# Second token half of x loaded a second time, transposed, with its root spread by one product, in a hybrid decoder layer

## The chip, the cores and the metric

The kernel runs on one core of a Trainium2 chip. The core has a matrix engine (TensorE, "PE" in the profile, with its weight loads as "PEld"), three engines for elementwise work (VectorE "DVE", ScalarE "ACT", GpSimd "POOL"), and queues that start transfers between device memory and the on-chip memory (here mostly that of SyncE, "SP"). Matrix products are written to a small accumulator memory, PSUM, of eight banks of 128x512 f32; everything else lies in SBUF, a memory of 128 partitions. The metric is device time of one execution in microseconds; the median of three runs is 1091.97 us (1091.26 to 1092.28).

## The reference

One decoder layer on x of 1024 tokens and width 1024 in float32. Cut to what matters here:

```python
h = rmsnorm(x, pre_w_mix) * (1.0 + sc1) + sh1          # sh1, sc1: columns of silu(c) @ w_ada + b_ada
proj = h @ w_in                                         # attention q, k, v and four recurrent inputs
aq, ak, av, hq, hf, hi, hg = split(proj)
attn = rmsnorm(window_attention(rope(aq), rope(ak), av, sinks), attn_out_w)
rec  = rmsnorm(hgrn2(silu(hq), 1 - f, hi, log f), hg_norm_w) * silu(hg)
x = x + g1 * rmsnorm(concat(attn, rec) @ w_out, post_w_mix)
# then a second sub-layer: a dense MLP of width 4096 with squared ReLU, normalised and modulated alike
```

`rmsnorm` divides a token's row by the root of its mean square, and `sc1`, `sh1` are one number per column of the width, the same for all tokens.

## The kernel before

**Tiles.** Tokens are cut into eight blocks of 128 (`tb`), in two halves `th` of four blocks each. The width is cut into eight blocks of 128 (`kb`). A product over the width needs h with the width on the partitions, while x arrives with tokens on the partitions. So each half is first multiplied row by row with its root (`norm_scale`, L207, one instruction for a token block and a half of the width), then transposed by TensorE against the identity (`first_T`, L215: four 128x128 transposes into one PSUM bank for a `kb`), and then taken out of PSUM by `split_evac` (L223). The matrix products run in a format with a shortened mantissa, so every factor is split into a high part and a rest, and a product is three matmuls (high x high, high x rest, rest x high). `split_evac` makes this split in a chain of three engines: ScalarE writes `hhi = a*xT + s` (a and s are the modulation's columns), GpSimd forms `f = hhi - s`, and VectorE writes `hlo = a*xT - f`.

**Order.** All compute instructions go through the helper `Queue` (L28), whose issuing line is L39; so all rows of the profile bear L39. While an engine is pinned (`pin(True, ...)`, L358, until L697), each instruction is tied behind the one issued before it on that engine: the engine's queue has the order of the program text. Behind L697 the framework's scheduler orders freely, but nothing gets ahead of the last pinned instruction.

**First half.** The loop over `kb` from 1 to 7 (L464) does for each block of the width: `first_evac` of the first half; `first_wq`, `first_wql`, `first_kv`, which split the weights of q and of k, v; the products `first_mm(kb, tb, part)` for token blocks 0 to 3, part 0 with hhi and part 1 with hlo, into the banks pq0 to pq3 and two shared banks for k and v; and `first_T` of the next block. Between them come the columns of the modulation: `mod_sum` (L309) adds a weight tile times a number of c on VectorE (rows `macc`), `mod_turn` (L318) transposes the sum on TensorE (rows `pmt`, in the bank of `a_ps`), reduces it and writes the columns that the next blocks' `split_evac` read. At `kb == 3` SP's queue gets the loads of token blocks 4 to 7, two tiles for a block (a half of the width each): eight loads of 256 KB. Their squares (`norm_sq`, rows `jx`, ScalarE) follow at `kb` 5 and 6, the root (`norm_rstd`) at 6, the row scalings at 6 and 7, the first two transposed blocks of the second half at 7.

**PSUM.** `tp_ps` hands out five banks, `mm_ps` two and `a_ps` one. During the first half four of the five and both of `mm_ps` hold sums; one of the five is left for transposes, and `a_ps` serves the modulation.

**Second half.** A loop at L678 and L682 issues `first_evac(1, kb, first_T(1, kb))`, the copies of the finished q blocks (`qproj`) and of k, v (`kvproj`), and the products of token block 4's q (`pq4`), three steps behind the evacuations. Then come the rotations (`rope`) and, from L730, a list of sixteen pieces (`filler`): q and k, v of token blocks 4 to 7 and the values of the recurrent part, between which the attention steps of the token blocks are placed. Attention of block 0 begins before piece 4, that is behind the q and k, v products of blocks 4 and 5.

Of the kernel before, what the change touches and what calls it, by code (L numbers as in the profile page):

```python
# [47 lines left out]
def hybrid_layer(ctx: ExitStack, tc: tile.TileContext, I, out, dbg=None):  # L48
# [40 lines left out]
    def mm_ps(name):  # L89
        return pmm.tile([P, 512], F32, tag="mm", name=name)  # L90
# [124 lines left out]
    def first_T(th, kb, mk=tp_ps):  # L215
        pst = mk(f"xT{th}_{kb}")
        hf, col = kb // 4, (kb % 4) * P
        for j in range(4):
            PE.transpose(pst[:, j * P:(j + 1) * P], xh[th * 4 + j][hf][:, col:col + P], ident)
        return pst  # L220
# [147 lines left out]
    def idle(n):  # L368
        for _ in range(n):
            PE.matmul(spare_ps, lhsT=ones_r, rhs=spare, start=True, stop=True)  # L370
# [6 lines left out]
    def first_rows(*js):  # L377
        for j in js:
            PE.transpose(xT0[0][:, j * P:(j + 1) * P], xh[j][0][:, 0:P], ident)
# [31 lines left out]
    def first_wql(kb):  # L411
        hi, lo = wq[kb]
        DVE.tensor_tensor(lo, wqr[kb], hi.bitcast(F32), ALU.subtract)
# [26 lines left out]
    norm_scale(0, 0, ACT, (3,))  # L440
    idle(4)
    mod_mm((0, 1), range(2))
    first_rows(2)
    idle(1)
    first_rows(3)
    mod_mm((0, 1), range(2, 4))
    mod_copy((0, 1))
    first_part(1)
# [5 lines left out]
        first_mm(0, tb, 0, (0,))  # L454
    mod_fold((0, 1))
    first_wql(1)
    for tb in (2, 3):
        first_mm(0, tb, 0, (1,))
    xT0.append(first_T(0, 1))
    for tb in (2, 3):  # L460
        first_mm(0, tb, 1)

    nextq = {1: (1, 0)}
    for kb in range(1, KB):  # L464
        q = nextq.get(kb)
        first_evac(0, kb, xT0[kb])
        if kb + 1 < KB:
            first_wq(kb + 1)
        if kb == 3:
            norm_scale(0, 1, ACT)  # L470
            pin(True, SP)
            for hf in range(2):
                for tb in range(4, TB):
                    load_x(tb, (hf,))
            pin(False, SP)
        first_mm(kb, 0, 0)
        first_mm(kb, 1, 0)
        if q:
            mod_mm(q)
            mod_copy(q)  # L480
        first_mm(kb, 2, 0)
        if kb in (3, 5):
            mod_turn((kb // 2 + 1, 0))
        first_mm(kb, 3, 0)
        if kb + 1 < KB:
            first_wql(kb + 1)
        if q:
            mod_fold(q)
        if kb == 2:
            mod_sum((2, 0), (2, 6, 3, 7))  # L490
        if kb == 4:
            mod_sum((3, 0), (5, 2, 6, 3, 7))
        if kb in (1, 3, 5):
            first_kv((kb + 1) // 2, DVE)
        if kb == 1:
            mod_sum((2, 0), (0, 4, 1, 5))
        if kb == 3:
            mod_sum((3, 0), (0, 4, 1))
        if kb + 1 < KB:
            xT0.append(first_T(0, kb + 1))  # L500
        if kb in (5, 6):
            for tb in range(4, TB):
                norm_sq(tb, (kb - 5,))
        if kb == 6:
            norm_rstd(1, 0, 4)
            norm_scale(1, 0, DVE)
        if kb == 7:
            norm_scale(1, 1, DVE)
        if kb == KB - 1:
            xT1 = [first_T(1, 0), first_T(1, 1, a_ps)]  # L510
        for tb in range(4):
            first_mm(kb, tb, 1)

# [8 lines left out]
    def htok(tb):  # L522
        sl = slice(tb % 4 * P, tb % 4 * P + P)
        return [(hh[k][tb // 4][0][:, sl], hh[k][tb // 4][1][:, sl]) for k in range(KB) if hh[k][tb // 4]]
# [6 lines left out]
    sinT = cload("sinT", [P, TB, 16], pool=XA)  # L531

    def qproj(tb):
        if tb < 5:
            pq = pq0[tb]
        else:
            pq = mm_ps(f"pq{tb}")
            proj3(pq, htok(tb), wq)
        q = m_(f"q{tb}")
        if tb in (0, 1):  # L540
            DVE.tensor_scalar(q, pq, 0.125, None, ALU.mult)
        else:
            ACT.activation(q, pq, AF.Copy, scale=0.125)
        qn.append(q)

    def kvproj(tb):
        if tb < 4:
            pk = pk0[tb]
        else:
            pk = mm_ps(f"pk{tb}")  # L550
            proj3(pk[:, :256], htok(tb), wkv)
        kv = XA.tile([P, 256], F32, tag="kv", bufs=8, name=f"kv{tb}")
        if tb < 4:
            DVE.tensor_copy(kv, pk[:, :256])
        else:
            ACT.activation(kv, pk[:, :256], AF.Copy)
        kvn.append(kv)

    def rope(tb, nh, eng=POOL):
# [115 lines left out]
            next(att[tb])  # L675

    att = [attention(tb) for tb in range(TB)]
    for kb in range(2):  # L678
        qproj(kb)
        first_evac(1, kb, xT1[kb])  # L680
    pq0.append(mm_ps("pq4"))
    for kb in range(2, KB + 3):  # L682
        if kb < KB:
            first_evac(1, kb, first_T(1, kb, mm_ps if kb == 2 else tp_ps))
        if kb == 2:
            qproj(2)
            qproj(3)
        if kb == KB:
            for tb in range(4):
                kvproj(tb)  # L690
        if kb > 2:
            proj3(pq0[4], htok(4)[kb - 3:kb - 2], wq[kb - 3:kb - 2], kb == 3, kb == KB + 2)
    for tb in range(4):
        eng = DVE if tb < 2 else POOL
        rope(tb, 8, eng)
# [1046 lines left out]
def layout(x, c, w_ada, b_ada, pre_w_mix, w_in, attn_sinks, attn_out_w, lb_table,  # L1742
           hg_norm_w, w_out, post_w_mix, pre_w_mlp, w_up, w_down, post_w_mlp):
    A = {}
    f = lambda a: np.ascontiguousarray(a)
    cols = lambda v: f(np.asarray(v).reshape(-1, P).T)
    A["x"] = f(np.asarray(x)[0])
    t_cT = cols(np.asarray(c)[0])
    wa = np.asarray(w_ada)[0]
    w1 = wa[:, :2048]  # L1750
    A["wada1"] = f(w1.reshape(4, 2, P, 2, 4, 256).transpose(3, 4, 0, 2, 1, 5).reshape(2, 4, 4, P, 512))
    A["wada1"][:, 2:] = (w1.reshape(2, 4, P, 2, 4, 256)[:, :, :, :, 2:].transpose(0, 4, 1, 2, 3, 5)
                         .reshape(2, 2, 4, P, 512))
    A["wada1"][:, 0] = (w1.reshape(2, 2, 2, P, 2, 8, P)[:, :, :, :, :, :2].transpose(1, 5, 0, 3, 4, 2, 6)
                        .reshape(2, 4, P, 512))
    A["wada"] = f(wa.reshape(KB, P, 6, 2, 512).transpose(2, 3, 0, 1, 4))
    ba = np.asarray(b_ada)[0]
    t_bT = cols(ba)
    A["b_g1"] = f(ba[2048:3072])
    A["b_g2"] = f(ba[5120:6144])  # L1760
    t_prew1 = cols(np.asarray(pre_w_mix)[0])
    t_prew2 = cols(np.asarray(pre_w_mlp)[0])
    A["postw1"] = f(np.asarray(post_w_mix)[0])
    A["postw2"] = f(np.asarray(post_w_mlp)[0])
    wi = np.asarray(w_in)[0]
    perm = [0, 4, 1, 5, 2, 6, 3, 7]
    A["w_q"] = f(wi[:, :512].reshape(D, 8, 64)[:, perm].reshape(KB, P, 512))
    A["w_kv"] = f(wi[:, 512:768].reshape(4, 2, P, 256).transpose(0, 2, 1, 3).reshape(4, P, 512))
    A["w_hv"] = f(wi[:, 1792:2304].reshape(KB, P, 512))
    hd = np.stack([wi[:, 1280:1792], wi[:, 768:1280], wi[:, 2304:2816]])  # L1770
    A["w_hd"] = f(hd.reshape(3, KB, P, 4, P).transpose(3, 0, 2, 1, 4).reshape(4, 3, P, D))
    sk = np.asarray(attn_sinks)[0]
    order = [0, 1, 4, 5, 2, 3, 6, 7]
    A["sinks"] = f(np.broadcast_to(sk[order], (P, 8)))
    A["attw"] = f(np.asarray(attn_out_w)[0].reshape(8, 64)[perm].reshape(4, P).T)
    A["lbt"] = f(np.asarray(lb_table).reshape(2, 4, P).transpose(2, 0, 1))
    A["hgw"] = f(np.asarray(hg_norm_w)[0].reshape(P, 1))
    wo = np.asarray(w_out)[0]
    A["w_o"] = f(np.concatenate([wo[:512].reshape(8, 64, D)[perm].reshape(4, P, D), wo[512:].reshape(4, P, D)]))
    A["w_u"] = f(np.asarray(w_up)[0].reshape(KB, P, 32, P).transpose(2, 1, 0, 3).reshape(32, P, D))  # L1780
    A["w_dn"] = f(np.asarray(w_down)[0].reshape(32, P, D))
    A["tab"] = f(np.concatenate([np.eye(P, dtype=np.float32), t_cT, t_bT, t_prew1, t_prew2], 1))
    inv = (np.float64(500000.0) ** (-np.arange(0, 16, 2) / 16.0)).astype(np.float32)
    ang = (np.arange(1024, dtype=np.float32)[:, None] * inv[None, :]).astype(np.float64)
    co, si = np.cos(ang).astype(np.float32), np.sin(ang).astype(np.float32)
    A["cosT"] = f(np.concatenate([co, co], 1).reshape(TB, P, 16).transpose(1, 0, 2))
    A["sinT"] = f(np.concatenate([-si, si], 1).reshape(TB, P, 16).transpose(1, 0, 2))
    i = np.arange(P)
    A["mle"] = (i[None, :] <= i[:, None]).astype(np.int32)
    A["fle"] = (i[:, None] <= i[None, :]).astype(np.float32)  # L1790
    si_, ti = i[:, None], i[None, :]
    A["hmask"] = (si_ <= ti).astype(np.int32)
    A["rmask"] = f(np.broadcast_to((np.arange(512) % CH != 0).astype(np.float32), (P, 512)))
    return A
# [14 lines left out]
```

## Time and profile before

| | |
|---|---|
| runs | 1091.26, 1091.97, 1092.28 us (median 1091.97) |
| profiled execution, its own time | 1091.43 us |
| its span in the profile | 1089.5 us |
| granted TensorE clock | 0.998 |
| PE busy | 1072.7 us, 98% |
| DVE busy | 803.2 us, 74% |
| ACT busy | 586.2 us, 54% |
| POOL busy | 373.0 us, 34% |
| bytes moved | 203.63 MB in the span |

A row of the time-ordered view has the start in us, the duration, engine, line, operation, the tile written and the tiles read, the shape, the count; in brackets stands how long the engine was idle before and what ended that. A row of the chain of waits has start, duration, engine and tile. A row of the windows has for each engine the busy time in the window and the number of instructions (PE, PEld, DVE, ACT, POOL), then the granted clock, the DMA share and GB/s. Matmuls overlap their neighbours, so the time between starts says more than a matmul's own duration.

### The profile page before, as it was taken

Reading aid. Unit: us, or ns where it says so; the run is one execution under the profiler, and the core shown is the slowest. Engines: PE = TensorE matmul, PEld = TensorE weight load, DVE = VectorE, ACT = ScalarE, POOL = GpSimd, SP = SyncE. Lnnn points to the kernel's source line nnn. Section 1 sums busy time; section 2 is a strip of 40 time slices with the busy share of each in tenths; the row PEclk is TensorE's granted clock in tenths of the full one; section 3 lists DMA queues with packets and bytes.
Section 4 is the critical chain, followed back from the end, with each engine's and each line's share of the span. In section 5 each row is a group of like instructions: output and inputs, shape, how many; then the busy total and the mean of one; then the engine's idle time right before and its main releaser. Section 6 shows DMA issues by size and latency. Waiting matters only on the chain.

```text
span 1089.5 us, 16106 instructions
## 1 busy us (share of the span) xinstructions
PE 1072.7 (98%) x5480; PEld 875.2 (80%) x5480; DVE 803.2 (74%) x1336; ACT 586.2 (54%) x1207; POOL 373.0 (34%) x497
## 2 busy tenths in 40 slices
PE   8999999999999999999999999999999999999996
PEld 6888666788888888888888888888888888888885
DVE  4867768878865564559777767776777787899786
ACT  4535553454565754566655555556664544466435
POOL 1263211143234653432444434444333334300014
PEclk9999999999999999999999999999999999999999
DMA  9701201544310252324577776767999888998538
GB/s 359 264 20 65 92 1 59 167 130 124 115 59 30 88 196 85 135 87 137 194 248 244 234 258 213 264 232 248 315 377 300 274 287 276 321 303 272 172 95 140
DMA packets 101826, 203.63 MB, mean 187 GB/s; under 512 B 13040, under 2 KB 13808, under 8 KB 101744
## 3 DMA queue, kind: packets, MB, share of 16 engines
q1 hardware_dynamic: 86256, 155.04, 41.9%
q0 software_dynamic: 15200, 47.20, 14.4%
q8 instruction: 43, 0.70, 0.3%
q14 instruction: 39, 0.32, 0.1%
q10 hardware_dynamic: 288, 0.36, 0.1%
HBM read 147.51 MB, written 55.05 MB: 186 GB/s over the span
## 4 chain that ended last, share of the span: by engine, by line
PE 90%; DVE 4%; DMA 2%; ACT 1%; POOL 1%; issue 1%; DVEq 0%; SPq 0%; POOLq 0%; ACTq 0%
PE pda L39 16%; PE pua L39 14%; PE pdc L39 8%; PE po L39 8%; PE puc L39 7%; PE pu L39 4%; PE pdb L39 4%; PE phg L39 4%; PE phq L39 3%; PE pub L39 3%; PE phf L39 3%; PE pv L39 3%; PE pq L39 3%; PE pk L39 1%; PE o L39 1%; PE sc L39 1%
## 5 line engine op out<-in xcount | busy, mean ns | idle before, releaser
L39 POOL TENSOR_TENSOR b<-b,b 128x512 f32<-128x512 f32 x64 | 88.7, 1386 | 216.4 <-DMA b<-w_dn 216.0
L39 ACT ACTIVATE dw<-dwr 128x512 fp32r<-128x512 f32 x72 | 45.4, 631 | 53.2 <-DMA dwr<-td 30.1
L39 ACT ACTIVATE s<-s 128x512 f32<-128x512 f32 x84 | 53.0, 631 | 31.8 <-DVE s L39 30.5
L39 DVE TENSOR_TENSOR acc<-pda,acc 128x512 f32<-128x512 f32 x68 | 46.7, 686 | 19.6 <-PE pda L39 19.2
L39 DVE TENSOR_TENSOR dw<-dwr,dw 128x512 fp32r<-128x512 f32 x72 | 53.1, 737 | 5.8 <-ACT dw L39 5.7
L39 POOL TENSOR_TENSOR rrf<-ssf,mhalf 128x1 f32<-128x1 f32 x7 | 7.6, 1081 | 105.5 <-DVE ssf L39 105.5
L39 POOL DMA_DIRECT2D td<-b x64 | 36.4, 568 | 19.0 <-POOL b L39 19.0
L39 ACT ACTIVATE s<-pua 128x512 f32<-128x512 f32 x28 | 16.7, 597 | 40.2 <-PE pua L39 37.4
L39 ACT ACT_TABLE_LOAD x28 | 35.9, 1283 | 1.7 <-PEq L1802 1.2
L39 DVE TENSOR_TENSOR wt<-a,wt 128x512 fp32r<-128x512 f32 x42 | 35.3, 841 | 0.9 <-ACT wt L39 0.9
L39 DVE TENSOR_TENSOR wt<-s,wt 128x512 fp32r<-128x512 f32 x42 | 34.2, 814 | 2.3 <-ACT wt L39 2.2
L39 DVE SCALAR_TENSOR_TENSOR macc<-wada,cs,macc 128x512 f32<-128x512 f32 x42 | 33.6, 800 | 3.1 <-DMA wada<-wada 2.6
L39 POOL DMA_DIRECT2D b<-w_dn x64 | 34.5, 541 | 2.7 <-issue 2.7
L39 POOL TENSOR_TENSOR comb<-comb,rd 128x512 f32<-128x512 f32 x8 | 11.7, 1458 | 63.3 <-DVE rd L39 44.2
L39 PE MATMUL pua<-bt_0h,wt 128*128 128x512 f32 x84 | 32.7, 389 | 0.0
L39 PE MATMUL pua<-bt_1h,wt 128*128 128x512 f32 x84 | 32.7, 389 | 0.0
L39 PE MATMUL pua<-bt_2h,wt 128*128 128x512 f32 x84 | 32.7, 389 | 0.0
L39 PE MATMUL pua<-bt_3h,wt 128*128 128x512 f32 x84 | 32.7, 389 | 0.0
L39 ACT ACTIVATE wt<-s 128x512 fp32r<-128x512 f32 x42 | 26.3, 627 | 7.6 <-DVE s L39 7.4
L39 DVE TENSOR_TENSOR acc<-pdc,acc 128x512 f32<-128x512 f32 x36 | 24.6, 684 | 7.2 <-PE pdc L39 7.0
L39 PE MATMUL pda<-dw,du_6h 128*128 128x512 f32 x96 | 29.6, 389 | 0.0
L39 PE MATMUL pdc<-dw,du_3h 128*128 128x512 f32 x96 | 29.5, 389 | 0.0
(766 smaller groups left out, 3746.5 us busy)
## 6 DMA issues: line engine op xcount, KB each, us to landing
dur<-ud SPq DMA_DIRECT2D x112, 256.0 KB, 4.4
wada<-wada SPq DMA_DIRECT2D x64, 256.0 KB, 3.6
b<-w_dn POOLq DMA_DIRECT2D x64, 256.0 KB, 5.2
td<-b POOLq DMA_DIRECT2D x64, 256.0 KB, 3.4
dwr<-td SPq DMA_DIRECT2D x64, 256.0 KB, 4.4
a<-w_u SPq DMA_DIRECT2D x56, 256.0 KB, 4.5
dwr<-w_dn SPq DMA_DIRECT2D x48, 256.0 KB, 4.3
ud<-s SPq DMA_DIRECT2D x42, 256.0 KB, 3.4
```

What stands on the lines that cost most here:

```text
L39: ins = op(*args, **kw)
```

## The change

The input is laid out twice: besides `x`, device memory holds `xT1`, the second token half with the width on the rows, as eight tiles of 128x512. The kernel loads these eight tiles (256 KB each) on SP's queue at `kb` 5 and 6 and no longer transposes or scales the rows of token blocks 4 to 7. The untransposed tiles of these blocks are still loaded, since their squares give the root. The root, one number for a token, now has to be multiplied along the free dimension: VectorE writes `dgx`, the identity times the root, four 128x128 blocks; one product of a matrix of ones with it puts the root of each of the 512 tokens on every partition (`rbx`, in PSUM); and VectorE multiplies each `xT1[kb]` with it in place, just ahead of that block's `first_evac`.

With that come a new order in the first half: the transposes of block 1 stand one group of products earlier; blocks 3, 5 and 7 of the width are transposed into the bank of `a_ps`; the modulation's sums are dealt out otherwise over the blocks (the last of gate 2 at `kb == 3`); one warming product is left out; six of the eight squares stand at `kb` 5 and two at 6. In the second half the loop has one form for all eight blocks: product, evacuation, one copy of q or k, v (all on ScalarE now), and the three matmuls each of token blocks 4 and 5, where pq5 stood among the pieces behind.

```diff
@@ -440,9 +440,7 @@
-    first_rows(2)
-    idle(1)
-    first_rows(3)
+    first_rows(2, 3)
...
     first_wql(1)
+    xT0.append(first_T(0, 1))
     for tb in (2, 3):
         first_mm(0, tb, 0, (1,))
-    xT0.append(first_T(0, 1))
...
-        first_mm(kb, 0, 0)
-        first_mm(kb, 1, 0)
+        if kb == 3:
+            mod_sum((2, 0), (7,))
+        if kb in (3, 5):
+            first_wql(kb + 1)
+        for tb in range(3):
+            first_mm(kb, tb, 0)
+            if kb == 7 and tb == 1:
+                rbx = tp_ps("rbx")
+                PE.matmul(rbx, lhsT=ones, rhs=dgx.rearrange("p a t -> p (a t)"), start=True, stop=True)
         if q:
             mod_mm(q)
             mod_copy(q)
-        first_mm(kb, 2, 0)
         if kb in (3, 5):
             mod_turn((kb // 2 + 1, 0))
         first_mm(kb, 3, 0)
-        if kb + 1 < KB:
+        if kb not in (3, 5) and kb + 1 < KB:
             first_wql(kb + 1)
...
-        if kb == 2:
-            mod_sum((2, 0), (2, 6, 3, 7))
-        if kb == 4:
-            mod_sum((3, 0), (5, 2, 6, 3, 7))
...
-        if kb == 1:
-            mod_sum((2, 0), (0, 4, 1, 5))
-        if kb == 3:
-            mod_sum((3, 0), (0, 4, 1))
+        if kb < 5:
+            mod_sum(*{1: ((2, 0), (0, 4, 1)), 2: ((2, 0), (5, 2, 6, 3)),
+                      3: ((3, 0), (0, 4, 1)), 4: ((3, 0), (5, 2, 6, 3, 7))}[kb])
         if kb + 1 < KB:
-            xT0.append(first_T(0, kb + 1))
+            xT0.append(first_T(0, kb + 1, a_ps if kb in (2, 4, 6) else tp_ps))
+        for tb, hf in {5: ((4, 0), (5, 0), (6, 0), (7, 0), (4, 1), (5, 1)), 6: ((6, 1), (7, 1))}.get(kb, ()):
+            norm_sq(tb, (hf,))
         if kb in (5, 6):
-            for tb in range(4, TB):
-                norm_sq(tb, (kb - 5,))
+            for j in range(4 * kb - 20, 4 * kb - 16):
+                xT1.append(load_raw(hT_ if j < 6 else m_, f"xT1_{j}", I["xT1"][j]))
         if kb == 6:
             norm_rstd(1, 0, 4)
-            norm_scale(1, 0, DVE)
-        if kb == 7:
-            norm_scale(1, 1, DVE)
-        if kb == KB - 1:
-            xT1 = [first_T(1, 0), first_T(1, 1, a_ps)]
+            dgx = t_("dgx", (P, 4, P))
+            DVE.tensor_tensor(dgx, ident.unsqueeze(1).broadcast_to([P, 4, P]),
+                              rx[1].unsqueeze(2).broadcast_to([P, 4, P]), ALU.mult)
...
-    for kb in range(2):
-        qproj(kb)
+    pq0.append(a_ps("pq4"))
+    for kb in range(KB):
+        DVE.tensor_tensor(xT1[kb], xT1[kb], rbx, ALU.mult)
         first_evac(1, kb, xT1[kb])
-    pq0.append(mm_ps("pq4"))
-    for kb in range(2, KB + 3):
-        if kb < KB:
-            first_evac(1, kb, first_T(1, kb, mm_ps if kb == 2 else tp_ps))
-        if kb == 2:
-            qproj(2)
-            qproj(3)
-        if kb == KB:
-            for tb in range(4):
-                kvproj(tb)
-        if kb > 2:
-            proj3(pq0[4], htok(4)[kb - 3:kb - 2], wq[kb - 3:kb - 2], kb == 3, kb == KB + 2)
+        (qproj if kb < 4 else kvproj)(kb % 4)
+        if kb == 0:
+            pq0.append(mm_ps("pq5"))
+        for tb in (4, 5):
+            proj3(pq0[tb], htok(tb)[kb:kb + 1], wq[kb:kb + 1], kb == 0, kb == KB - 1)
...
+    A["xT1"] = f(np.asarray(x)[0, 512:].T.reshape(KB, P, 512))
```

More of the change, by code (lines that the diff above doesn't have):

```diff
@@ L463, in hybrid_layer @@
     nextq = {1: (1, 0)}
+    xT1 = []
     for kb in range(1, KB):
@@ L533, in qproj @@
     def qproj(tb):
-        if tb < 5:
+        if tb < 6:
             pq = pq0[tb]
@@ L539, in qproj @@
         q = m_(f"q{tb}")
[L540 to L543, printed above, removed]
+        ACT.activation(q, pq, AF.Copy, scale=0.125)
         qn.append(q)
@@ L552, in kvproj @@
         kv = XA.tile([P, 256], F32, tag="kv", bufs=8, name=f"kv{tb}")
[L553 to L556, printed above, removed]
+        ACT.activation(kv, pk[:, :256], AF.Copy)
         kvn.append(kv)
```

## The prediction, made before the result was known

> **What bounds the kernel now.** I read the page first (busy shares), then the stages by window, then the chain of waits between 53 and 81 us, and last the time-ordered rows of each engine in that stretch.
>
> ```profile
> span 1089.5 us, 16106 instructions
> PE 1072.7 (98%) x5480; PEld 875.2 (80%) x5480; DVE 803.2 (74%) x1336; ACT 586.2 (54%) x1207; POOL 373.0 (34%) x497
> ...
> 45.00:50.00 5.00, 4.42 (x28) 3.79 (x28) 4.24 (x11) 3.38 (x10) 0.83 (x1) 1.00 0.28 90
> 55.00:60.00 5.00, 4.66 (x34) 4.10 (x33) 4.09 (x8) 2.03 (x3) 1.37 (x2) 1.00 0.00 0
> ...
> 100.00:110.00 10.00, 9.64 (x79) 7.86 (x78) 9.25 (x20) 4.89 (x16) 3.83 (x7) 1.00 0.45 152
> 110.00:120.00 10.00, 8.80 (x67) 6.32 (x67) 7.58 (x18) 5.67 (x21) 3.43 (x7) 1.00 0.64 217
> 125.00:200.00 75.00, 73.50 (x432) 51.66 (x429) 58.47 (x121) 33.05 (x110) 13.07 (x18) 1.00 0.14 44
> ```
>
> TensorE is the bound: 16.8 us of idle in the whole span (1089.5 − 1072.7). A microsecond taken from it, or put into it as a wait, before 200 us moves the end by about that much, except for what the idle time of the attention stage gives back: 0.36 + 1.20 + 1.50 = 3.1 us in the last three rows. The changed stretch, in the chain of waits:
>
> ```profile
> 53.89 0.46 PE pq L39 x2
> ...
> 56.68 0.87 PE xT L39 x8
> ...
> 57.90 0.23 PE pq L39
> ...
> 66.58 0.76 DVE hlo L39
> 67.34 0.04 issue
> 67.39 1.20 PE pq L39 x4
> 68.58 2.88 PE pk L39 x24
> 71.46 5.46 PE pq L39 x24
> 76.92 2.87 PE pk L39 x24
> 79.80 0.44 PE pqT L39 x4
> ```
>
> At 53.89 block 7 of the first half begins; eight transposes for the second half follow at 56.68 (six more groups of four come up to 65). pq4 ends at 68.58, then kv4 (2.88), pq5 (5.46), kv5 (2.87), and attention starts at 79.80. Without kv4, "pq4 and pq5 are done" would stand at 76.92 − 2.88 = **74.04**; in the changed kernel kv4 comes after both, so this is the point to compare.
>
> **The change, part by part.** *Removed from TensorE:* 32 transposes. By the row of 56.68, eight take 0.87: 4 × 0.87 = 3.48 us. Also one warming product of 0.23 (the step from 16.45 to 16.68 in the chain):
>
> ```profile
> 16.45 0.23 PE spare L39
> 16.68 0.12 PE xT L39
> ...
> 1079.05 1.02 PE L39 MATMUL pdly<-x,c_tab 128*128 128x512 f32 x2
> ```
>
> *Added to TensorE:* the product that spreads the root, 128x512 with plain f32 operands; no row before has that form with `ones`, the last row is the same shape and type: 1.02 busy, of which I take 0.95 as its step. Bounds 0.47 (two passes at the 0.23 of an fp32r matmul) and 1.02. On work alone the change is worth 3.48 + 0.23 − 0.95 = 2.8 us. pq5 only moves.
>
> *The eight row scalings* leave VectorE, but eight products of the same size come in, `xT1[kb] * rbx`. What decides is where they stand. The loop issues, for each kb: the product (VectorE), hhi (ScalarE), f (GpSimd), hlo (VectorE). VectorE is pinned there, so the product of kb+1 sits in its queue behind hlo of kb, and hlo of kb waits for f, f for hhi, hhi for the product of kb. Nothing of kb+1 can begin before kb is through. Today VectorE has only hlo in this chain, and the transposes run ahead. These rows show that the queue does keep its order, and what each link takes:
>
> ```profile
> 57.82 0.69 DVE L39 TENSOR_SCALAR q<-pq 128x512 f32<-128x512 f32 x1 [0.59 <-PE pq L39]
> 58.83 0.75 DVE L39 SCALAR_TENSOR_TENSOR hlo<-xT,a,f 128x512 fp32r<-128x512 f32 x1 [0.32 <-POOL f L39]
> 59.50 0.68 DVE L39 TENSOR_SCALAR q<-pq 128x512 f32<-128x512 f32 x1
> ...
> 61.02 0.75 DVE L39 SCALAR_TENSOR_TENSOR hlo<-xT,a,f 128x512 fp32r<-128x512 f32 x1 [0.18 <-POOL f L39]
> ...
> 105.75 0.67 DVE L39 TENSOR_TENSOR q<-q,rb 128x512 f32<-128x512 f32 x1
> ...
> 59.42 0.78 ACT L39 ACTIVATE hhi<-xT,sh,a 128x512 fp32r<-128x512 f32 x1 [0.82 <-PE xT L39]
> ...
> 60.29 0.69 POOL L39 TENSOR_SCALAR f<-hhi,ns 128x512 f32<-128x512 f32 x1 [0.82 <-ACT hhi L39]
> ...
> 33.06 2.55 ACT L39 ACTIVATE x<-x,r_x 128x512 f32<-128x512 f32 x4
> ```
>
> VectorE stood 0.32 us before the hlo of 58.83 while the copy queued behind it, q1, had its sum finished already (last pq1 matmul, 57.90 + 0.23 = 58.13 in the chain): an in-order queue. The period of one kb: product 0.67 (the row of 105.75, same shape with one operand in PSUM) + 0.02 of handing over; hhi until f starts 60.29 − 59.42 = 0.87 from PSUM, and since xT1 now lies in SBUF, where four scalings took 2.55 (0.61 each, against a step of about 0.67), I take 0.80; f until hlo 61.02 − 60.29 = 0.73; hlo until the next VectorE instruction 59.50 − 58.83 = 0.67. Together **P = 2.89 us**, eight times: 7 × 2.89 + (0.69 + 0.80 + 0.73 + 0.76 + 0.04) = 20.23 + 3.02 = **23.25 us**. TensorE's work in it is 48 matmuls of 5.46 / 24 = 0.23, 1.4 us a kb: it stands idle half of each period, and being pinned too, with kv4 and kv5 behind the loop, has nothing to fill in.
>
> *Where the chain starts.* The product with `ones` stands in block 7 behind two token blocks (each two pq and two pk matmuls, 0.46 + 2 × 2.88 / 24 = 0.70), so, if block 7 begins as before at 53.89, the first VectorE product starts at 53.89 + 1.40 + 0.95 = **56.24**, hlo of block 7 being done by then. End of the chain 56.24 + 23.25 = 79.49; four matmuls remain after the last hlo, 1.20 by the row of 67.39: **80.69**. Against 74.04: **+6.65 us**.
>
> *That block 7 begins as before* is a term of its own. The reordering takes waits away from TensorE and brings two:
>
> ```profile
> 20.64 0.50 PE L39 MATMUL pq<-wq1h,hhi 128*128 128x512 f32 x1 [0.17 <-ACT hhi L39]
> ...
> 31.17 0.66 PE L39 MATMUL xT<-c_tab,x 128*128 128x128 f32 x4 [0.31 <-DVE hlo L39]
> ...
> 41.30 0.66 PE L39 MATMUL xT<-c_tab,x 128*128 128x128 f32 x4 [0.20 <-DVE hlo L39]
> ...
> 46.03 0.66 PE L39 MATMUL pmt<-c_tab,macc 128*128 128x128 f32 x4 [0.58 <-DVE macc L39]
> ...
> 31.63 3.42 DVE L39 SCALAR_TENSOR_TENSOR macc<-wa,cs,macc 128x512 f32<-128x512 f32 x4
> ...
> 45.89 0.75 DVE L39 SCALAR_TENSOR_TENSOR hlo<-xT,a,f 128x512 fp32r<-128x512 f32 x1
> ...
> 47.88 0.78 ACT L39 ACTIVATE hhi<-xT,sh,a 128x512 fp32r<-128x512 f32 x1 [1.62 <-PE xT L39]
> ```
>
> Taken away: 0.17 + 0.31 + 0.20 and the 0.23, some 0.9, since xT now changes bank with `a_ps`. Brought: in block 3 the modulation's transposes (pmt) need the last macc, which now stands behind hlo of block 3 (the four macc end at 31.63 + 3.42 = 35.05; 0.67 for hlo and about 0.8 for the fifth come behind), and in block 5 pmt takes the bank that xT of block 5 holds until hlo (45.89 + 0.75 = 46.64, against 46.03): about a microsecond of waiting each, against 0.58 now. I put the net at 0, with bounds −1.5 (all waits gone) and +1.0. The two more squares that ScalarE does in block 5 (0.61 each, as its scalings) lie in the 1.62 it idles before hhi of block 6; without that cover they would cost 1.2. The q and kv copies that move to ScalarE (some 0.6 each, as its scalings) lie in the 2 us that it waits in each period of 2.89.
>
> *The eight loads* of 256 KB go on SP's queue behind the eight of x:
>
> ```profile
> 34.45 5.01 SPq L39 DMA_DIRECT2D x<-x  x8
> ```
>
> Eight issues take 5.0 us, so those of xT1 keep SP until some 45 and land by 50, in a DMA share that falls to 0.28 (45 to 50) and 0.00 (55 to 60); the first is read at 56.24. Cost nothing; behind them the small tables and the w_hv loads come 5 us later, and nothing of these is read inside the loop. If SP held them until the x buffers were free (about 50), the first would still land by 56, and the rest faster than one per 2.89.
>
> **The sum** against the profiled execution: 1091.43 + 6.65 = 1098.1. Its own time stands 0.54 below the median, so against the median 1091.97 + 6.65 = **1098.6**.
>
> **Rivals.** *Clock.* TensorE would stand still about 1.5 us in each period, for 23 us. The end of the span shows what idling does to the granted clock:
>
> ```profile
> 1080.20 1.12 PE L39 MATMUL pdly<-ga,dg 128*128 128x512 f32 x2
> ...
> 1080.00:1085.00 5.00, 1.20 (x3) 0.30 (x2) 4.00 (x9) 1.77 (x6) 0.93 (x1) 0.92 0.96 249
> 1085.00:1089.50 4.50, 0.00 (x0) 0.00 (x0) 0.00 (x0) 0.00 (x0) 0.00 (x0) 0.50 0.18 69
> ...
> 1.65 4.60 PE L39 MATMUL spare<-spare,ones_r 128*128 128x512 f32 x11 [1.65 <-DVE spare L121]
> ```
>
> The last matmul ends at 1081.3; 0.92 on average, with 0.50 as the floor, is 0.8 us at half, so the clock fell some 2.9 us after it, twice a gap of this loop. The Trainium skill ("TensorE: Matmul & The Clock Gate", What's actually happening) says that the clock halves after an idle window of about 3.4 us; with that rule, and the trace agrees roughly, 1.5 us gaps cost nothing. The same page (A second HAM failure mode: psum-queue depth-cycling) says that frequent short idling between groups of matmuls can make the gate swing as well; by it this rival holds. Should the clock be halved, six matmuls (2.8 us) still fit in a period; the four after the last hlo take 0.9 more, and kv4 starts at half rate: at the start of the kernel 11 products took 4.60, 0.42 each instead of 0.23, so up to half of 4.6 is lost. +6.65 + 0.9 + 2.3 = +9.9: 1101.8. Chance 0.13.
>
> *Given back later.* Attention now starts at 80.69 + 5.75 = 86.4 instead of 79.80, but VectorE's, ScalarE's and GpSimd's other work need not all be late. If TensorE's idle 3.1 us between 100 and 200 closes up, +3.5 is left: 1095.5. Against it: those waits are on attention's own chain, which starts from TensorE. Chance 0.15.
>
> *It gets faster.* One mechanism: the products run ahead of hlo, in the queue of VectorE, so that the links of different kb overlap. Then a period is TensorE's own 1.40 (VectorE needs 0.67 + 0.67, ScalarE two operations of some 0.65), and pq5 ends at 53.89 + 2.81 (block 7, four of 0.70) + 0.95 + 1.40 (its second part) + 48 × 0.234 = 70.3, 3.8 before 74.04: 1088.2. It decides from where P falls under about 2 us: 56.24 + 7P + 3.0 + 1.2 = 74.04 gives P = 1.94. For it speaks that no row shows this loop; against it the row of 58.83, and that each of four links has its duration in a row. Chance 0.08.
>
> **How the numbers follow.** Forecast 0.64, clock 0.13, given back 0.15, faster 0.08. The forecast's own range: P between 2.70 (an estimate: hhi at the 0.61 of the scalings plus its 0.09 of handing over, the product at 0.6) and 3.15 (hhi at its 0.87, f slower by a quarter) gives −1.5 to +2.1, the start −1.5 to +1.0, seldom at the same end: 1096 to 1101. The range for 8 in 10 takes in the clock's case and most of what is given back: 1094.5 to 1102. This kernel's runs spread by 0.1%, so 0.2% (2.2 us) is about what can be told from no change: faster 0.07, within it 0.04 (a gain cut short, or more given back than I see), slower 0.89.
>
> **What would show it.** In the changed profile: xT1 products, hhi, f and hlo in strict turn on VectorE, about 2.9 us from product to product, between some 56 and 79; TensorE's rows of pq in that loop in groups of six with a wait for hlo and hhi each, a share near one half in windows of 5 us; pk for token block 4 starting near 80.7 and pqT near 86; a wait of about 1 us before each pmt; a granted clock of 1.00 there. Two products without an hlo between them, or a period below 2 us, would prove me wrong; so would a late first product (loads, or the root).

## The result

| | before | changed |
|---|---|---|
| median | 1092.12 us (6 runs, 1091.26 to 1092.96) | 1099.48 us (6 runs, 1099.10 to 1100.90) |
| profiled execution, own time | 1091.43 us | 1099.29 us |
| its span | 1089.5 us | 1097.5 us |
| granted clock | 0.998 | 0.998 |

The change makes the kernel slower: ratio 1.007, 95% interval 1.006 to 1.0081, or 7.4 us by the medians and 7.9 us by the two profiled executions. Forecast were 1098.6 us and a range of 1094.5 to 1102.0.

The page of the changed kernel, its first lines, and then the windows of the changed stretch (columns as before: busy time and count of PE, PEld, DVE, ACT, POOL, granted clock, DMA share, GB/s):

```profile
span 1097.5 us, 16056 instructions
PE 1072.3 (98%) x5449; PEld 870.8 (79%) x5449; DVE 804.9 (73%) x1331; ACT 589.8 (54%) x1213; POOL 372.6 (34%) x497
...
60.00:65.00 5.00, 3.22 (x11) 1.40 (x9) 1.66 (x3) 2.55 (x4) 1.39 (x2) 1.00 0.00 0
65.00:70.00 5.00, 3.13 (x10) 1.64 (x10) 2.38 (x4) 2.09 (x4) 0.69 (x1) 1.00 0.00 0
70.00:75.00 5.00, 2.93 (x9) 1.53 (x10) 2.42 (x4) 1.38 (x4) 1.39 (x2) 1.00 0.00 0
75.00:80.00 5.00, 3.53 (x12) 1.67 (x11) 1.63 (x3) 2.17 (x4) 1.33 (x2) 1.00 0.00 0
...
110.00:120.00 10.00, 9.36 (x71) 7.20 (x71) 8.07 (x19) 6.12 (x24) 3.04 (x6) 1.00 0.71 215
120.00:130.00 10.00, 9.08 (x69) 7.29 (x67) 8.77 (x20) 3.98 (x12) 3.43 (x7) 1.00 0.45 155
```

TensorE's busy time is 0.4 us lower than before (1072.3 against 1072.7), and its span is 8.0 us longer. The busy time alone hides how much work went: a matmul that stands alone behind a wait is recorded as longer (0.50 us, against 0.39 to 0.40 in a row of them), and the run with one block ahead, below, shows 1069.8 for the same 5449 matmuls. Between 60 and 80 us no engine is busy throughout: TensorE 2.9 to 3.5 of 5 us, VectorE, ScalarE and GpSimd less than that, DMA nothing. That is the look of a chain which passes from engine to engine. Its rows for two blocks, VectorE first, then ScalarE and GpSimd:

```profile
62.33 0.68 DVE L39 TENSOR_TENSOR xT<-xT,rbx 128x512 f32<-128x512 f32 x1
64.69 0.75 DVE L39 SCALAR_TENSOR_TENSOR hlo<-xT,a,f 128x512 fp32r<-128x512 f32 x1 [1.67 <-POOL f L39]
65.35 0.68 DVE L39 TENSOR_TENSOR xT<-xT,rbx 128x512 f32<-128x512 f32 x1
67.77 0.75 DVE L39 SCALAR_TENSOR_TENSOR hlo<-xT,a,f 128x512 fp32r<-128x512 f32 x1 [1.73 <-POOL f L39]
68.44 0.68 DVE L39 TENSOR_TENSOR xT<-xT,rbx 128x512 f32<-128x512 f32 x1
...
63.05 0.81 ACT L39 ACTIVATE hhi<-xT,sh,a 128x512 fp32r<-128x512 f32 x1 [1.80 <-DVE xT L39]
...
66.13 0.81 ACT L39 ACTIVATE hhi<-xT,sh,a 128x512 fp32r<-128x512 f32 x1 [1.78 <-DVE xT L39]
...
63.95 0.69 POOL L39 TENSOR_SCALAR f<-hhi,ns 128x512 f32<-128x512 f32 x1 [2.33 <-ACT hhi L39]
...
67.04 0.69 POOL L39 TENSOR_SCALAR f<-hhi,ns 128x512 f32<-128x512 f32 x1 [2.39 <-ACT hhi L39]
```

Product 62.33, hhi 63.05, f 63.95, hlo 64.69, next product 65.35: strictly one after the other, 3.02 us, and 3.09 for the block behind. VectorE waits 1.7 us for f before each hlo, with the next product queued behind. Where the chain begins and ends; then TensorE's waits (total, times, longest), the first two from 55 to 82 us, the last two of the whole span:

```profile
56.21 0.69 DVE L39 TENSOR_TENSOR xT<-xT,rbx 128x512 f32<-128x512 f32 x1 [1.30 <-PE rbx L39]
...
80.10 0.76 DVE hlo L39
80.86 0.04 issue
80.91 1.20 PE pq L39 x4
82.10 5.74 PE pk L39 x48
87.85 0.44 PE pqT L39 x4
...
PE pq L39 <- DVE hlo L39: 6.0, 7, 0.9
PE pq L39 <- ACT hhi L39: 2.1, 7, 0.3
...
PE pmt L39 <- DVE hlo L39: 1.0, 1, 1.0
PE pmt L39 <- DVE macc L39: 0.9, 1, 0.9
```

In the loop of the second half TensorE waits for hlo and for hhi in seven of eight blocks, 8.1 us in all. Attention (pqT is its first product) starts at 87.85 instead of 79.80, 8.05 us later, and the span is 8.0 us longer: what was lost by then reaches the end whole.

### The profile page after: what moved, and what is told of

Its sections match the earlier page's. It is cut to its first block, busy times and chain, and to the rows that moved or that the text cites. A ratio compares the mean times of both kernels' runs of the same rounds, so it can differ in the third digit from the quotient of the medians.

```text
span 1097.5 us, 16056 instructions
## 1 busy us (share of the span) xinstructions
PE 1072.3 (98%) x5449; PEld 870.8 (79%) x5449; DVE 804.9 (73%) x1331; ACT 589.8 (54%) x1213; POOL 372.6 (34%) x497
## 4 chain that ended last, share of the span: by engine, by line
PE 86%; DVE 4%; ACT 1%; POOL 1%; issue 1%; DMA 0%; DVEq 0%; ACTq 0%; POOLq 0%
PE pda L39 16%; PE pua L39 14%; PE pdc L39 8%; PE po L39 8%; PE puc L39 7%; PE pu L39 4%; PE pdb L39 4%; PE phg L39 4%; PE phq L39 3%; PE pub L39 3%; PE phf L39 3%; PE pv L39 3%; PE o L39 1%; PE sc L39 1%; PE pq L39 1%; PE oT L39 1%
## 5 line engine op out<-in xcount | busy, mean ns | idle before, releaser
L39 DVE TENSOR_TENSOR dw<-dwr,dw 128x512 fp32r<-128x512 f32 x72 | 55.4, 769 | 9.1 <-ACT dw L39 9.0
L39 DVE TENSOR_TENSOR wt<-s,wt 128x512 fp32r<-128x512 f32 x42 | 37.2, 885 | 2.5 <-ACT wt L39 2.4
L39 DVE TENSOR_TENSOR s<-puc,s 128x512 f32<-128x512 f32 x14 | 9.7, 690 | 29.1 <-issue 26.7
L39 POOL TENSOR_SCALAR f<-hhi,ns 128x512 f32<-128x512 f32 (+1 forms) x17 | 12.3, 726 | 54.7 <-ACT hhi L39 51.1
```

Of the source, the lines that this page charges most:

```text
L39: ins = op(*args, **kw)
```

## The experiments

Three theories were put to the test. A: the loss is the order of VectorE's queue. B: it is the length of the links or other work in the loop, above all the copies that moved to ScalarE. C: a good part of it lies in the first half, with its new waits of pmt and the spreading product.

**Products one block ahead.** The changed kernel with only the place of the products altered:

```diff
+    def root_x(kb):
+        if kb < KB:
+            DVE.tensor_tensor(xT1[kb], xT1[kb], rbx, ALU.mult)
+
+    for kb in range(1):
+        root_x(kb)
     for kb in range(KB):
-        DVE.tensor_tensor(xT1[kb], xT1[kb], rbx, ALU.mult)
+        root_x(kb + 1)
         first_evac(1, kb, xT1[kb])
```

> The changed kernel with the eight products of the second half issued one block ahead: product 0, product 1, hlo 0, product 2, hlo 1 and so on; nothing else differs. Theory A (the loss is the order of VectorE's queue, which ties the product of a block behind hlo of the block before): hhi, f and hlo of neighbouring blocks overlap, the step from product to product falls from 3.08 to about 1.4 us, TensorE's 48 products run without waits (48 x 0.234 = 11.2 us), pqT starts near 76 instead of 87.85, and the time is 1088 to 1089. Theory B (the links themselves are too slow, or the copies on ScalarE hold hhi up): the step stays above 2.5 and the time above 1097. Theory C (a good part of the loss lies in the first half, in the two waits of pmt of 0.91 and 1.01 us and in the spreading product): pqT starts near 78 or later and the time stays at 1090 or above.

Measured: 1088.58 us (9 runs, 1088.36 to 1089.33), ratio to before 0.9972 (0.9962 to 0.9982). The busy times, VectorE's rows and, from the chain of waits, the end of the loop:

```profile
PE 1069.8 (98%) x5449; PEld 871.7 (80%) x5449; DVE 803.1 (74%) x1331; ACT 588.6 (54%) x1213; POOL 372.3 (34%) x497
...
56.24 1.28 DVE L39 TENSOR_TENSOR xT<-xT,rbx 128x512 f32<-128x512 f32 x2 [1.31 <-PE rbx L39]
58.60 0.75 DVE L39 SCALAR_TENSOR_TENSOR hlo<-xT,a,f 128x512 fp32r<-128x512 f32 x1 [1.08 <-POOL f L39]
59.27 0.68 DVE L39 TENSOR_TENSOR xT<-xT,rbx 128x512 f32<-128x512 f32 x1
...
62.30 0.68 DVE L39 TENSOR_TENSOR xT<-xT,rbx 128x512 f32<-128x512 f32 x1
...
71.32 5.74 PE pk L39 x48
77.07 0.44 PE pqT L39 x4
```

The same instructions in another order are 10.9 us faster by the medians, and attention starts 10.8 us earlier. TensorE no longer waits in the loop (8.1 us before) and is busy 2.5 us less in the whole span; against the kernel before it is busy 2.9 us less, close to the 2.8 that the prediction put on the work. Theory A stands and B falls; attention starts below the 78 that theory C asked for. The step is not quite the forecast 1.4: two products (59.27 to 62.30) take 3.03 us, just the length of one chain, so with one product ahead two blocks share a chain, 1.52 us each, and TensorE's products end at 71.32 instead of 70.3.

**One link shortened.** f of the second half on VectorE, which is quicker at it, though it adds to the busier engine:

```diff
-        POOL.tensor_scalar(hs, hi.bitcast(F32), n_col, 1.0, ALU.add, ALU.mult)
+        (eng or POOL).tensor_scalar(hs, hi.bitcast(F32), n_col, 1.0, ALU.add, ALU.mult)
...
-        split_evac(pst, a1[:, c], sh1[:, c], ns1[:, c], *hh[kb][th], f"f{th}_{kb}")
+        split_evac(pst, a1[:, c], sh1[:, c], ns1[:, c], *hh[kb][th], f"f{th}_{kb}",
+                   eng=DVE if th else None)
```

> The changed kernel with f of the second half (hhi minus s) computed by VectorE instead of GpSimd; order as in the changed kernel. This shortens one link of the chain and adds work to VectorE. Theory A (a serial chain of product, hhi, f, hlo): the period goes from 3.08 to 0.72 + 0.86 + 0.50 + 0.67 = 2.75, eight times 0.33 less: 2.6 us faster than the changed kernel, about 1096.9. If it were the load of VectorE rather than the chain, eight more instructions of 0.41 would make it 3.3 us slower: 1102.8.

Measured: 1097.38 us (4 runs, 1096.91 to 1097.61), 2.1 us under the changed kernel. The rows of one period on VectorE:

```profile
58.81 0.68 DVE L39 TENSOR_TENSOR xT<-xT,rbx 128x512 f32<-128x512 f32 x1
60.37 0.49 DVE L39 TENSOR_SCALAR f<-hhi,ns 128x512 f32<-128x512 f32 x1 [0.88 <-ACT hhi L39]
...
61.56 0.68 DVE L39 TENSOR_TENSOR xT<-xT,rbx 128x512 f32<-128x512 f32 x1
...
79.72 5.74 PE pk L39 x48
85.45 0.44 PE pqT L39 x4
```

The step is 61.56 − 58.81 = 2.75 us here and in each of the first three blocks, as worked out from the links; in the four behind it is 2.81 or 2.82, since product until hhi takes 0.78 there and not 0.71. Attention starts 2.4 us earlier, of which 0.16 is an earlier start of the loop (56.05), so the gain came out as 2.1 by the medians where 2.6 was expected. Eight more instructions on VectorE made the kernel faster: not its load but the length of the chain counts.

**The copies taken out.** Seven of the eight copies of q and k, v on ScalarE stand behind the loop:

```diff
-        (qproj if kb < 4 else kvproj)(kb % 4)
         if kb == 0:
+            qproj(0)
             pq0.append(mm_ps("pq5"))
...
     for tb in range(4):
+        if tb:
+            qproj(tb)
+        kvproj(tb)
```

> The changed kernel with seven of the eight q and k, v copies on ScalarE moved behind the loop of the second half (the first stays, since its bank is needed). Theory A: ScalarE's copies fill time in which it waits anyway; period 3.0 to 3.1 as before, time 1099.5 give or take 1. Theory B (the copies hold up hhi): the period falls by up to 0.58 in four blocks and 0.36 in four, up to 3.8 us: 1095.7.

Measured: 1099.83 us (4 runs, 1099.69 to 1100.70), the changed kernel's 1099.48 within its scatter. Two products of VectorE and the hhi between them:

```profile
65.30 0.68 DVE L39 TENSOR_TENSOR xT<-xT,rbx 128x512 f32<-128x512 f32 x1
...
68.39 0.68 DVE L39 TENSOR_TENSOR xT<-xT,rbx 128x512 f32<-128x512 f32 x1
...
66.08 0.81 ACT L39 ACTIVATE hhi<-xT,sh,a 128x512 fp32r<-128x512 f32 x1 [2.27 <-DVE xT L39]
```

3.09 us. ScalarE's copies are covered by its own waiting, as the prediction had them.

**The first half alone.** The kernel before with the new order of the first half, all else left (squares, transposes, scalings, the second half):

```diff
-    first_rows(2)
-    idle(1)
-    first_rows(3)
+    first_rows(2, 3)
...
+        if kb == 3:
+            mod_sum((2, 0), (7,))
...
-            xT0.append(first_T(0, kb + 1))
+            xT0.append(first_T(0, kb + 1, a_ps if kb in (2, 4, 6) else tp_ps))
```

> The kernel before with only the new order of the first half (no warming product, transposes of block 1 earlier, the bank of a_ps for blocks 3, 5 and 7, the modulation's sums dealt out anew); transposes and scalings of the second half, and the squares, as before. The prediction's step: the waits gained and lost cancel, block 7 begins near 53.9 and the time is that of before, 1092 give or take 0.6. Theory C: the two new waits of pmt come on top, 1093.5 to 1094. If the new order were a gain by itself: below 1091.3.

Measured: 1091.90 us (10 runs, 1091.39 to 1092.38) against 1091.83; ratio 1.0001 (0.9991 to 1.001). TensorE's rows, and behind them the row of the kernel before with which block 7 begins:

```profile
35.40 0.63 PE L39 MATMUL pmt<-c_tab,macc 128*128 128x128 f32 x4 [0.92 <-DVE macc L39]
...
46.32 0.65 PE L39 MATMUL pmt<-c_tab,macc 128*128 128x128 f32 x4 [1.01 <-DVE hlo L39]
...
54.01 0.40 PE L39 MATMUL pq<-wq7h,hhi 128*128 128x512 f32 x1
...
53.72 0.40 PE L39 MATMUL pq<-wq7h,hhi 128*128 128x512 f32 x1
```

The two waits of pmt are there, 1.9 us together, and yet block 7 begins only 0.3 later. They took the place of four waits of 1.26 us together (the 0.17, 0.31, 0.20 and 0.58 of the prediction's rows) and of the warming product of 0.23, so the two sides nearly cancel; in the changed kernel itself block 7 begins at 53.76. The interval allows this run about a microsecond either way, so the first half explains next to nothing of the 7.4 us, and theory C falls.

**Two blocks ahead.** `range(2)` and `root_x(kb + 2)` in the first diff.

> The changed kernel with the products issued two blocks ahead. In the run with one block ahead two products span one whole chain (product, hhi, f, hlo: 3.05 us), and the step was 1.52 to 1.57, half of it. Theory A goes on: with two ahead a step could be a third, 1.0, so TensorE's 1.40 a block becomes the bound; no wait of TensorE is left in the loop, the products of blocks 4 and 5 end at 70.2 to 70.4 instead of 71.32, and the time falls from 1088.6 by about 1.0 to 1087.6. If another engine sets the step at 1.5 (VectorE, or ScalarE with its copies), nothing changes: 1088.6.

Measured: 1088.05 us (6 runs, 1087.58 to 1088.51), ratio to before 0.9966 (0.9954 to 0.9979). From the chain of waits, and then one row each of VectorE and GpSimd:

```profile
65.57 5.29 PE pq L39 x22
70.86 5.75 PE pk L39 x48
76.61 0.44 PE pqT L39 x4
...
64.35 1.17 DVE L39 SCALAR_TENSOR_TENSOR hlo<-xT,a,f 128x512 fp32r<-128x512 f32 x1
...
61.86 3.12 POOL L39 TENSOR_SCALAR f<-hhi,ns 128x512 f32<-128x512 f32 x3 [0.25 <-ACT hhi L39]
```

The products end at 70.86 and attention starts at 76.61, 0.46 earlier than with one block ahead, although the spreading product began 0.23 later in this execution (55.41 against 55.18): 0.7 us, short of the forecast 0.9 to 1.1. By the times alone, 1088.05 against 1088.58, the two can't be told apart, since their intervals overlap. From 59 to 66 us TensorE is busy 6.93 of 7 us and VectorE 6.88, so the step is at the bound of both; whether a third of the chain, 1.02 us, could be reached with two blocks ahead, this run can't show. The links don't keep their lengths either: three f take 3.12 us and one hlo 1.17, where each took 0.69 and 0.75 in strict turn.

**Two blocks ahead, pmt later.** In addition, `mod_turn` behind `first_mm(kb, 3, 0)` instead of ahead of it.

> Two blocks ahead, and the modulation's transposes (pmt) of blocks 3 and 5 issued behind the product group of token block 3 instead of ahead of it, which gives TensorE 0.70 us of work in each of the two waits of 0.92 and 1.00. If these waits are what the first half loses: they fall to 0.2 and 0.3, block 7 begins 1.4 earlier, and the time is 1.4 lower than two blocks ahead alone, about 1086.2. If the columns that pmt makes come too late for the next block instead (hhi waits for them), the gain is given back there: 1087.6.

Measured: 1087.97 us (6 runs, 1087.47 to 1089.79), ratio to before 0.9968 (0.9956 to 0.998): no gain over two blocks ahead. TensorE's rows tell where part of it went:

```profile
35.10 0.63 PE L39 MATMUL pmt<-c_tab,macc 128*128 128x128 f32 x4 [0.21 <-DVE macc L39]
...
37.77 0.50 PE L39 MATMUL pq<-wq4h,hhi 128*128 128x512 f32 x1 [0.20 <-ACT hhi L39]
...
45.93 0.66 PE L39 MATMUL pmt<-c_tab,macc 128*128 128x128 f32 x4 [0.47 <-DVE hlo L39]
...
48.63 0.51 PE L39 MATMUL pq<-wq6h,hhi 128*128 128x512 f32 x1 [0.20 <-ACT hhi L39]
```

The waits of pmt fall from 0.91 and 1.01 to 0.21 and 0.47, 1.24 us less, but the next blocks' hhi, which needs the columns that pmt makes, is now late, and TensorE waits for it twice, 0.40 us. Block 7 begins 0.65 earlier than with two blocks ahead (53.37 against 54.02), where 1.4 was forecast, and 0.32 of that was there when block 1 began (20.12 against 20.44), ahead of the moved instructions. So the wait moved on in part, as the second alternative of the expectation had it; what is left of the gain, some 0.3 us, is too small for the medians to show.

## Why the prediction was right, point by point

*The chain.* Its mechanism, VectorE's in-order queue holding the product of a block behind hlo of the block before, is shown by the run with one product ahead, which takes away this order and nothing else, and by the run with f on VectorE, which shortens one link.

*Where it starts.* Forecast 56.24, measured 56.21: block 7 began as before (53.76 against 53.72 in the time-ordered rows). The spreading product stepped in 0.86 (from 55.34 in the chain of the run with one block ahead), with 0.04 until VectorE began, where 0.95 stood.

*Its period* is the term that was mis-sized: 2.89 forecast, (77.69 − 56.21) / 7 = 3.07 measured, with the last product at 77.69:

```profile
77.69 0.68 DVE L39 TENSOR_TENSOR xT<-xT,rbx 128x512 f32<-128x512 f32 x1
```

hlo to product (0.67) and f to hlo (0.73) came out as taken. The step "since xT1 now lies in SBUF I take 0.80" was wrong: hhi until f took 0.90 or 0.91 (once 0.98), longer than the 0.87 from PSUM. f waits until hhi has ended (0.81, and 0.09 of handing over), and 0.61 was the step between scalings of another form, not the time until one of them has ended. And product until hhi took 0.71 to 0.78 where 0.69 was put. The chain was 24.70 us (56.21 to 80.91) instead of 23.25, and these 1.45 us are the miss at the start of attention, expected at 86.4 and measured at 87.85; the profiled execution took 1099.29 us where the sum gave 1098.1, 1.2 more.

*The end.* The four last matmuls took 1.20 as by the row of before, kv4 and kv5 5.74.

*The first half at 0.* Right within what can be seen, and shown by the run of it alone: the two waits of about a microsecond came as told (1.9 us), and 1.5 us of older waits and the warming product went.

*The loads at nothing.* Right in the sum, but not as told. SP issued them from 45.90 to 49.65, behind the small tables and the first two w_hv tiles and not ahead, and the DMA share stayed high until 54 (0.90 from 53 to 54, 0.21 from 54 to 55). The first product waited for rbx, not for a load. The load of its own tile, issued at 45.90, had landed some five microseconds before (these loads took 3.2 to 5.0 us from issue to landing), but the last of the eight only one or two before, not six.

```profile
45.90 3.75 SPq L39 DMA_DIRECT2D xT<-xT  x8
...
53.00:54.00 1.00, 1.00 (x8) 0.86 (x7) 0.00 (x0) 0.33 (x1) 0.57 (x1) 1.00 0.90 346
54.00:55.00 1.00, 1.00 (x7) 0.86 (x6) 0.75 (x1) 0.00 (x0) 0.12 (x1) 1.00 0.21 70
```

*The rivals.* Clock: the granted clock was 1.00 in all windows of the loop, with two waits of TensorE in each period, up to 0.9 and 0.3 us, where the prediction had one of 1.5. By the Trainium skill ("TensorE: Matmul & The Clock Gate", What's actually happening) the gate falls after a window of about 3.4 us without work; the trace agrees as far as it goes, no gap here came near that. The swinging that the same page of the Trainium skill reports for frequent short idling (A second HAM failure mode: psum-queue depth-cycling) did not occur here, with these two waits in each 3.07 us. Given back later: no, 8.05 us at the start of attention and 8.0 at the end; TensorE idles 0.64 + 0.92 in the windows of 110 to 130 where before it idled 0.36 + 1.20 in those of 100 to 120, so the idle time of the attention stage moved along. Faster: that case needed the products ahead of hlo, at which 1088.2 was worked out; written that way, the kernel took 1088.6 with one block ahead and 1088.0 with two. So this rival was near the right sum for the kernel that the change could have been, though the products ended at 71.32 and 70.86 where it put 70.3: the times agree better than the terms do.

## What to carry to other kernels

When an engine's queue keeps program order and a block's work passes through it twice, with other engines in between, issue the first visit of the next blocks ahead of the second visit of this one; otherwise each block pays the whole chain, however idle all engines look. One first visit ahead halved the step here (3.07, then 1.52). That n of them would bring it to the chain over n + 1, until the busiest engine is the bound, is an extrapolation: with two ahead two engines were full already. And a row that saves work on the bounding engine tells nothing of the time before its replacement has been followed through every queue: here a change that takes some 2.8 us of work from TensorE cost 7.4 us, and the order of eight instructions was worth 10.9.

## What was not expected of the hardware

ScalarE's pass with a scale and a bias per partition took longer from SBUF (0.81) than from PSUM (0.78 before) at the same 128x512 f32, while scalings of the same size with a scale alone took 0.71 from SBUF. And with the copies out of the loop the wait from product to hhi still took 0.78 in most blocks (65.30 to 66.08), where some took 0.71. In the run with f on VectorE the chain of waits has a piece of ScalarE's sequencer (ACTq, 0.02 at 65.03) between product and hhi in the blocks with the longer wait and none in the first three; what this piece does was not tried, and neither was what stretches f and hlo when they overlap.
